# An opening that walks over k with normalised values at once, gate columns with token-major values, GLA states by one scan, and tiles at multiples of 256 bytes

## The chip, the cores and the metric

The kernel is one program on one core of a Trainium2 chip. The metric is the device time of one execution in microseconds (us). Of the kernel before, three runs took 1600.69, 1602.25 and 1602.29 us; their median is 1602.25 us.

## The reference

Two transformer blocks follow one another on 512 tokens (S) of width 1024 (D), all in fp32. The part that the change touches is the beginning of the first block:

```
mod = silu(c) @ ada_w + ada_b            # 6 x 1024: shift, scale, gain of two halves
sh_t, sc_t, g_t, sh_c, sc_c, g_c = split(mod)
h = rms_norm(x, tm_pre_g) * (1 + sc_t) + sh_t
y = token_mixer(h, w_in, ...)
x = x + g_t * rms_norm(y, tm_post_g)
h = rms_norm(x, cm_pre_g) * (1 + sc_c) + sh_c
x = x + g_c * rms_norm(conv_ffn(h, ...), cm_post_g)

token_mixer:  p = h @ w_in               # split in columns:
  mLSTM (q, k, v, o: 256 each; i, f: 4 each)
  GLA   (q, k, v, r: 256 each; a: 16):  log_a = log_sigmoid(a @ w_a2 + bias) / 16
        chunked: state = decay * state + k_dec^T v ; o = q_dec state + masked(q k^T) v
  conformer convolution (512: value and gate), short convolution (3 x 256)
  4 x 1024 gates; merged = sum of gate * (branch @ its output matrix); merged @ w_o
```

The second block (pooling, sparse attention over keys that an indexer picks, a second FFN with a convolution, a last norm) is the same in both kernels.

## The kernel before

**Numbers and products.** The values stand feature-major: 128 features on the partitions, 512 tokens along the row, 8 such blocks for the 1024 features. A product in fp32 is made of three in the faster fp32r format: every weight tile of 128x1024 is loaded raw (512 KB), rounded to `hi` by ScalarE (L120), and the rest `lo = raw - hi` is made by VectorE (L121); the activations have such a pair too (`hh`, `hl`). `mm3` then issues three matmuls: hi with hh (L132), hi with hl (L133), lo with hh (L134). One column block of 128 output columns is 8 blocks of k times 3, so 24 matmuls of 128x512.

**Order.** The program is written as a sequence; a framework with priorities orders each engine's instructions when the program is built, and they run in that order on each engine. `wload` gives loads and splits a higher priority, so that they stand ahead of the products; its buffers (`raw`, `hi`, `lo`) are three deep. SyncE issues all DMAs one after the other; where a buffer isn't free yet, the queue of SyncE waits, and everything behind it too.

**Opening (L347 to L458).** `c` is broadcast to all partitions by a DMA, and its silu makes `cb`. `ada_st(i)` loads a 128x1024 piece of ada_w into one of four `sraw` buffers and reduces it against `cb` on VectorE (L358), which gives 128 values of mod. A first loop over the 8 blocks j of k loads scale piece `ada[8+j]`, x and one weight column block, makes `gcols` (gain times 1+scale) and the pair xg = x times gain, not normalised and without shift, and multiplies it with the first four column blocks (gq0, gq1, gk0, gk1), whose splits stay in `wst`. The row sums of x squared run beside it (ScalarE squares, VectorE adds, L392); `rx`, the reciprocal root of every token's mean, is there after the eighth x, and scales these four results afterwards. A second loop loads the shift pieces `ada[j]`, makes the real h (L439 to L441), and multiplies it with the next four blocks (ifa, ca0, cg0, ca1); one shift piece (j = 1) is reduced by matmuls instead of VectorE (L433). The shift that the first four blocks lack is made by 16 matmuls of the shift with `wst` (L450, L451), and added later from `shw`.

**Gates, GLA and mLSTM.** The column block `ifa` holds 4 columns of i, 4 of f and 16 of a. From it come `i_sb`, `b_sb`, `d_sb` (mLSTM) and log_a (GLA), by Abs, Exp and Ln on ScalarE. The values gv and mv are made token-major, by 96 matmuls of 128x256 each (`gemm_t`, L158). For each p of two (two heads), the states of GLA's 16 chunks are a chain on VectorE: 15 operations of 128x64 (L615, L617), each on the one before. `vx` are copies of v by chunk (VectorE, L605).

**Post.** After the product with w_o the class `Post` adds up squares and products for the post-norm (L291 to L305), with working tiles `sq` of three rows.

## Time and profile before

| | |
|---|---|
| median of 3 runs | 1602.25 us |
| the profiled execution: time, span | 1601.86 us, 1600.1 us |
| mean granted clock of TensorE, as a share of full speed | 0.995 |
| PE, DVE, ACT, POOL busy | 98%, 67%, 42%, 1% |
| mean DMA rate | 110 GB/s |

The span runs from the first to the last instruction; 1.76 us of the execution lie around it. PE is TensorE, DVE VectorE, ACT ScalarE, POOL GpSimd, SP SyncE. A matmul's duration in the trace holds its way through the pipeline, and matmuls overlap; what a matmul costs in a row of them is the distance between two starts. A busy share over the whole span says little of a single stage, so the table is read together with the same shares in short stretches.

### The profile page before, as it was taken

How to read it: one execution, taken by the hardware profiler on the slowest of the kernel's cores; microseconds unless marked ns; L12 is line 12 of the kernel's file. 1: busy time of each engine (PE TensorE's matmuls, PEld its weight loads, DVE VectorE, ACT ScalarE, POOL GpSimd, SP SyncE). 2: the span in 40 equal slices, each digit the busy share in tenths (PEclk: the TensorE clock that was granted, in tenths of full speed). 3: DMA queues.
4: the chain of work that ended last, by engine and by line, in shares of the span. 5: the costliest groups of instructions: out<-in, count | busy, mean ns of one | idle time of the engine just before them, and what ended most of it. 6: DMA issues, size and time to landing. Idle time of an engine off the chain costs nothing.

```text
span 1600.1 us, 20699 instructions
## 1 busy us (share of the span) xinstructions
PE 1567.1 (98%) x8015; PEld 1314.9 (82%) x8015; DVE 1073.7 (67%) x1928; ACT 674.7 (42%) x1028; POOL 16.2 (1%) x43
## 2 busy tenths in 40 slices
PE   6999999999999999999999999999999999999998
PEld 4778888888888988888899978888889988888886
DVE  7776896657768766565358899977556565665234
ACT  4366532223453543443244363448343444444122
POOL 0000100000000000000000000000000000000000
PEclk9999999999999999999999999999999999999999
DMA  8411335544541222223345212220241232232231
GB/s 307 169 53 65 108 119 184 184 167 155 178 146 41 80 92 103 95 93 96 98 132 171 94 67 87 85 93 27 80 154 58 79 101 98 92 105 80 98 113 53
DMA packets 50962, 175.90 MB, mean 110 GB/s; under 512 B 5920, under 2 KB 6192, under 8 KB 50864
## 3 DMA queue, kind: packets, MB, share of 16 engines
q1 hardware_dynamic: 50864, 174.58, 32.7%
q8 instruction: 63, 1.03, 0.3%
q14 instruction: 35, 0.29, 0.1%
HBM read 172.46 MB, written 2.10 MB: 109 GB/s over the span
## 4 chain that ended last, share of the span: by engine, by line
PE 90%; DVE 5%; ACT 2%; issue 1%; DMA 1%; SPq 0%; ACTq 0%; DVEq 0%
PE acc L132 22%; PE acc L133 22%; PE acc L134 22%; PE acc L198 3%; PE acc L1361 3%; PE tp L1361 2%; PE acc L158 1%; PE pc L1270 1%; PE pa L1361 1%; PE pb L1361 1%; PE pc L1361 1%; PE pa L198 1%; PE pb L198 1%; PE pc L198 1%; DVE lo L121 1%
## 5 line engine op out<-in xcount | busy, mean ns | idle before, releaser
L121 DVE TENSOR_TENSOR lo<-raw,hi 128x1024 fp32r<-128x1024 f32 (+1 forms) x245 | 296.4, 1210 | 326.1 <-ACT hi L120 315.8
L132 PE MATMUL acc<-hh,hi 128*128 128x512 f32 x1208 | 473.4, 392 | 0.0
L134 PE MATMUL acc<-hh,lo 128*128 128x512 f32 x1208 | 473.2, 392 | 0.0
L133 PE MATMUL acc<-hl,hi 128*128 128x512 f32 x1208 | 471.8, 391 | 0.0
L120 ACT ACTIVATE hi<-raw 128x1024 fp32r<-128x1024 f32 (+1 forms) x245 | 257.3, 1050 | 477.9 <-PE acc L133 360.8
L132 PEld LDWEIGHTS acc<-hh,hi 128*128 128x128 f32 x1208 | 227.1, 188 | 48.9 <-issue 2.2
L134 PEld LDWEIGHTS acc<-hh,lo 128*128 128x128 f32 x1208 | 227.2, 188 | 47.9 <-issue 0.9
L133 PEld LDWEIGHTS acc<-hl,hi 128*128 128x128 f32 x1208 | 227.1, 188 | 47.8 <-issue 1.4
L134 PE MATMUL acc<-act_h,lo 128*128 128x256 f32 (+1 forms) x242 | 80.3, 332 | 0.0
L133 PE MATMUL acc<-act_l,hi 128*128 128x256 f32 (+1 forms) x242 | 80.2, 331 | 0.0
L132 PE MATMUL acc<-act_h,hi 128*128 128x256 f32 (+1 forms) x242 | 80.1, 331 | 0.0
L120 ACT ACTIVATE act_h<-ffe 128x512 fp32r<-128x512 f32 x44 | 27.7, 630 | 104.2 <-DVE ffe L986 104.2
L268 DVE SCALAR_TENSOR_TENSOR raw<-raw,cb 128x1024 f32<-128x1024 f32 x32 | 39.1, 1223 | 36.7 <-DMA raw<-in_ada_dram 36.6
L982 DVE SCALAR_TENSOR_TENSOR ffe<-acc,vec,ffe 128x510 f32<-128x510 f32 x82 | 61.2, 748 | 2.6
L985 ACT ACTIVATE ffe<-ffe 128x512 f32<-128x512 f32 x44 | 27.8, 631 | 79.6 <-DVE ffe L982 79.6
L980 DVE SCALAR_TENSOR_TENSOR ffe<-acc,vec,ffe 128x511 f32<-128x511 f32 x82 | 60.7, 743 | 0.0
L133 PEld LDWEIGHTS acc<-act_l,hi 128*128 128x128 f32 x242 | 46.0, 190 | 4.4
L134 PEld LDWEIGHTS acc<-act_h,lo 128*128 128x128 f32 x242 | 46.0, 190 | 4.3
L132 PEld LDWEIGHTS acc<-act_h,hi 128*128 128x128 f32 x242 | 46.0, 190 | 4.2
L121 DVE TENSOR_TENSOR act_l<-ffe,act_h 128x512 fp32r<-128x512 f32 x44 | 30.4, 690 | 27.3 <-ACT act_h L120 27.3
L819 DVE SCALAR_TENSOR_TENSOR cv<-u,vec,cv 128x512 f32<-128x512 f32 x60 | 43.3, 745 | 0.0
L198 PE MATMUL acc<-hh,hi 128*128 128x256 f32 x144 | 40.4, 287 | 0.8 <-ACT hh L945 0.7
(635 smaller groups left out, 2752.0 us busy)
## 6 DMA issues: line engine op xcount, KB each, us to landing
raw<-in_up_dram SPq DMA_DIRECT2D x88, 512.0 KB, 3.2
raw<-in_wg_dram SPq DMA_DIRECT2D x48, 512.0 KB, 3.3
raw<-in_dn_dram SPq DMA_DIRECT2D x44, 512.0 KB, 3.5
raw<-in_w_dram SPq DMA_DIRECT2D x43, 512.0 KB, 3.4
raw<-in_ada_dram SPq DMA_DIRECT2D x32, 512.0 KB, 3.3
sraw<-in_ada_dram SPq DMA_DIRECT2D x16, 512.0 KB, 5.7
raw<-in_wo_dram SPq DMA_DIRECT2D x16, 512.0 KB, 3.3
raw<-in_dn_dram SPq DMA_DIRECT2D x11, 384.0 KB, 3.4
```

The lines of the kernel that those rows point to most:

```text
L120: A.activation(hi, src, AF.Copy)
L121: V.tensor_sub(lo, src, hi.bitcast(F32))
L132: T.matmul(out, wh_, ah, start=start, stop=False)
L133: T.matmul(out, wh_, al, start=False, stop=False)
L134: T.matmul(out, wl_, ah, start=False, stop=stop)
L198: T.matmul(a, w_, x_, start=(k == 0 and n == 0 and half == 0), stop=(k == KT - 1 and n == 2 and half == 1), skip_group_check=True)
L268: V.scalar_tensor_tensor(raw, raw, 1.0, cb, op0=ALU.mult, op1=ALU.mult, accum_out=mod[:, i:i + 1])
L819: V.scalar_tensor_tensor(cv[:, j], u0[:, j, k:k + 512], htap[:, 2 * k + j:2 * k + j + 1], cv[:, j], op0=ALU.mult, op1=ALU.add)
L980: V.scalar_tensor_tensor(t[:, 1:512], acc[:, 0:511], vcol(taps, 44 + i), t[:, 1:512], op0=ALU.mult, op1=ALU.add)
L982: V.scalar_tensor_tensor(t[:, 2:512], acc[:, 0:510], vcol(taps, i), t[:, 2:512], op0=ALU.mult, op1=ALU.add)
L985: A.activation(e[0], e[0], AF.Silu)
L1361: T.matmul(o, act[a][:, k, t], w[:, n0:n1], start=(k == 0 and i == 0), stop=(k == KF - 1 and i == 2), skip_group_check=True)
```

## The change

It has four parts.

1. **Opening.** A second copy of x, token-major (`xr`, four pieces of 128x1024, 512 KB each), is loaded first. ScalarE squares its rows with an accumulator, so the row sums `s0` come without VectorE, and `rx` is there before any product. `c` is spread over the partitions by 8 transposes on TensorE and not by a DMA. TensorE multiplies a tile of zeros (`warm`, 3 and 18 matmuls, and 3 on `rx`) in the meantime. `late1`, a one that depends on `rx`'s root, is an operand of the first two reductions. Then one loop over k: per step `ada[8+j]`, x, `ada[j]` and one weight tile are loaded. The weight tile now holds 128 rows of k for all eight column blocks (gq0, gq1, gk0, gk1, ca0, cg0, ca1, cg1), and its 24 matmuls go into eight PSUM banks. h is the final one from the start, so the shift's matmuls, `shw`, `wst`, the second loop and the reduction by matmuls go.
2. **Gate columns.** `ifa` isn't a column block any more; its 24 columns are appended to gv: `wgv`, 96 matmuls of 128x280, and four transposes bring the 24 columns back to feature-major. Exp and Ln run once over three rows.
3. **GLA.** The chain of 15 operations per p becomes one scan over 1024 elements (L593 of the changed kernel) on operands that ScalarE lays out; half of the `vx` copies go to ScalarE. The functions `states`, `chunk_scores`, `gla_out`, `gla_gate` are called in a new order, with the products mq, mk ahead of the GLA work, and gr, mv between its parts.
4. **Tiles.** Many tiles are allocated at multiples of 64 elements (256 bytes); `raw` is 1120 and `hi`, `lo` are 1152 long; `Post` after w_o uses ordinary 128x512 tiles and no `sq3`, and in the first FFN `sq3` has one buffer and not two.

```diff
@@ opening
-        nc.sync.dma_start(out=cb, in_=io["c"].broadcast_to([128, D]))
         nc.sync.dma_start(out=vec[:, 0:VSTART], in_=io["vec"][:, 0:VSTART])
-        A.activation(cb, cb, AF.Silu)
+        nc.sync.dma_start(out=ident, in_=io["cst"])
+        xr = st.tile([128, 4, 1024], F32, name="xr")
+        for b in range(4):
+            nc.sync.dma_start(out=xr[:, b], in_=io["xr"][b * 128:(b + 1) * 128])
+        def warm(n, x_):
+            for _ in range(n):
+                T.matmul(idle[:, 0:x_.shape[1]], ident if x_ is not zero else zero[:, 0:128], x_, start=True, stop=True)
+        warm(WARM[0], zero)
...
+        for n in range(2):
+            cp = bank(("pb", "pc")[n])
+            for k in range(4):
+                T.transpose(cp[:, k * 128:(k + 1) * 128], ccol[:, 4 * n + k:4 * n + k + 1].to_broadcast([128, 128]), ident)
...
+        warm(WARM[1], zero)
+        for b in range(4):
+            A.activation(xr[:, b], xr[:, b], AF.Square, accum_out=s0[:, b:b + 1])
+        y0 = rsqrt(s0, 1.0 / D, 4)
+        late1 = sm.tile([128, 49], F32, tag="late1", name="late1", bufs=1)[:, 0:1]
+        V.tensor_scalar(late1, y0[:, 0:1], 0.0, 1.0, op0=ALU.mult, op1=ALU.add)
+        rb = rowcast(y0)
+        A.activation(rx, rb, AF.Copy)
+        warm(3, rx[:, 0:256])
+        accs = [bank(t) for t in ("acc", "acc", "acc", "pc", "pa", "pb", "tp", "tp")]
+        for j in range(KT):
+            g, sh = gcols[:, 0, j:j + 1], mod[:, j:j + 1]
+            ada_st(8 + j, late1 if j == 0 else 1.0)
             nc.sync.dma_start(out=x0[:, j], in_=io["xT"][:, j])
...
+            ada_st(j, late1 if j == 0 else 1.0)
+            floor[0] = tc.cur_priority
+            w = wload(io["w1"][j])
             V.scalar_tensor_tensor(g, mod[:, 8 + j:9 + j], scb1[:, j:j + 1], vcol("tm_pre_g", j), op0=ALU.add, op1=ALU.mult)
+            V.tensor_tensor(sh, sh, vcol("ada_b", j), op=ALU.add)
             t = st.tile([128, 512], F32, tag="nt", name="nt", bufs=2)
+            V.scalar_tensor_tensor(t, x0[:, j], g, rb if j == 0 else rx, op0=ALU.mult, op1=ALU.mult)
             A.activation(h[0][:, j], t, AF.Identity, bias=sh)
             V.scalar_tensor_tensor(h[1][:, j], t, sh, h[0][:, j].bitcast(F32), op0=ALU.add, op1=ALU.subtract)
+            for m in range(NST):
+                sl = slice(m * 128, (m + 1) * 128)
+                mm3(accs[m], w[0][:, sl], w[1][:, sl], h[0][:, j], h[1][:, j], j == 0, j == KT - 1)
...
-            T.matmul(shp[0:2], shs[:, j], wk[0], start=(j == 0), stop=False, skip_group_check=True)
-            T.matmul(shp[0:1], shs[:, j, 0:1], wk[1], start=False, stop=(j == KT - 1), skip_group_check=True)
@@ gate columns
+        gemm_t([io["wgv"][n] for n in range(2)], h, [o[:, 0:NGV] for o in out], NGV)
...
+        for b in range(4):
+            T.transpose(ifa[0:80, b * 128:(b + 1) * 128], gt4[:, b], ident)
...
+        A.activation(rows[:, 2:5], rows[:, 2:5], AF.Exp, scale=-1.0)
+        A.activation(rows[:, 2:5], rows[:, 2:5], AF.Ln, bias=1.0)
@@ GLA
-                            V.scalar_tensor_tensor(sc_[:, cc + 1], sc_[:, cc], fcol[:, p, cc:cc + 1], kv[:, bi, c],
-                                                   op0=ALU.mult, op1=ALU.add)
+                A.activation(sc_[:, :, 8 * b2:8 * b2 + 8], kv.rearrange("p b c v -> p v (b c)"), AF.Copy)
+            fz = m4("fz")[:, 0:1024]
+            A.activation(fz.rearrange("p (v c) -> p v c", c=16), fcol[:, p].unsqueeze(1).to_broadcast([128, 64, 16]), AF.Copy)
+            V.tensor_tensor_scan(scf, fz, scf, 0.0, op0=ALU.mult, op1=ALU.add)
...
+        states(0)
+        chunk_scores(0)
+        ggate = [gla_gate(j) for j in range(2)]
+        gla_out(0)
+        states(1)
+        chunk_scores(1)
...
+        gemm_t([io["w1"][m], io["w1"][m + 1]], h, [out[b // 2][:, b % 2] for b in range(4)], 256)
...
+        gla_out(1)
@@ tiles
+    def padded(pool, shape, dtype=F32, **kw):
+        return pool.tile([shape[0], (shape[1] + 63) // 64 * 64], dtype, **kw)[:, 0:shape[1]]
-        raw = wr.tile([128, 1024], F32, tag="raw", name="raw")
+        raw = wr.tile([128, 1120], F32, tag="raw", name="raw")
-        post = Post(t2, lambda: m4("sq3")[:, 0:768].rearrange("p (n t) -> p n t", n=3), sums, x, y, gcols[:, 1])
+        post = Post(t2, None, [t2("th", 4) for _ in range(3)], x, y, gcols[:, 1])
-        post = Post(fe, lambda: f1.tile([128, 3, 256], F32, tag="sq3", name="sq3", bufs=2), sums, x, y, gcols[:, 3])
+        post = Post(fe, lambda: f1.tile([128, 3, 256], F32, tag="sq3", name="sq3", bufs=1), sums, x, y, gcols[:, 3])
```

How this moves instructions is seen in three places of the order of the engines.

TensorE at the start of the program, before (`wst` are the kept splits of the first column block, in the first loop):

```order
L132 MATMUL acc<-hh,wst_109 128x512
L133 MATMUL acc<-hl,wst_109 128x512
L134 MATMUL acc<-hh,wst_110 128x512
L132 MATMUL acc<-hh,wst_109 128x512
L133 MATMUL acc<-hl,wst_109 128x512
```

The same place of the changed kernel:

```order
L374 MATMUL acc<-zero 128x256 x5
L385 MATMUL pb<-cst,ccol 128x128 x4
L385 MATMUL pc<-cst,ccol 128x128 x4
L374 MATMUL acc<-zero 128x256 x16
L251 MATMUL tp<-cst,rs_y 128x128 x4
L374 MATMUL acc<-rx,cst 128x256 x3
L134 MATMUL acc<-hh,hi 128x512 x3
L134 MATMUL pc<-hh,hi 128x512
L134 MATMUL pa<-hh,hi 128x512
L134 MATMUL pb<-hh,hi 128x512
```

Ahead of the first product there now stand 21 matmuls on zeros (in two groups), the transposes that spread `c`, the four that spread the reciprocal roots, and three matmuls on `rx`.

VectorE in one step of the second loop, before (L358 is the reduction of a piece of ada_w, L439 to L441 make h):

```order
L437 TENSOR_TENSOR mod<-mod,vec 128x1
L439 SCALAR_TENSOR_TENSOR nt<-x_101,gcols,raw 128x512
L358 SCALAR_TENSOR_TENSOR sraw,mod<-sraw,cb 128x1024
L441 SCALAR_TENSOR_TENSOR hl<-nt,mod,hh 128x512
L437 TENSOR_TENSOR mod<-mod,vec 128x1
```

VectorE from the root's last operation to the end of the first step, after (L359 is the reduction, L123 the split of the weight):

```order
L237 SCALAR_TENSOR_TENSOR rs_y<-rs_u,rs_y 128x4
L398 TENSOR_SCALAR late_168<-rs_y 128x1
L359 SCALAR_TENSOR_TENSOR sraw,mod<-sraw,late_168,cb 128x1024 x2
L411 SCALAR_TENSOR_TENSOR gcols<-mod,scb_117,vec 128x1
L412 TENSOR_TENSOR mod<-mod,vec 128x1
L414 SCALAR_TENSOR_TENSOR nt<-x_101,gcols,tp 128x512
L123 TENSOR_TENSOR lo<-raw,hi 128x1024
L416 SCALAR_TENSOR_TENSOR hl<-nt,mod,hh 128x512
```

A step now has two reductions and a split where the old second loop had one reduction, and the first step's reductions stand behind the root.

VectorE among the states of GLA, before (L617 is one link of the chain, L605 a copy of v):

```order
L615 COPY x1a<-pc 128x64
L605 COPY x1a<-gv 32x2x64
L617 SCALAR_TENSOR_TENSOR x1a<-x1a,fcol,pc 128x64
L605 COPY x1a<-gv 32x2x64
L617 SCALAR_TENSOR_TENSOR x1a<-x1a,fcol,pc 128x64
```

The corresponding place after (L593 is the scan):

```order
L584 COPY x1a<-gv 32x2x64 x4
L695 TENSOR_TENSOR mx_548<-x2a,mx_548 4x512
L603 COPY_PREDICATED x2a<-x2a,pa 128x512
L603 COPY_PREDICATED x2a<-x2a,pb 128x512
L584 COPY x1a<-gv 32x2x64 x4
L593 SCALAR_TENSOR_TENSOR x1a<-fz,x1a 128x1024
L123 TENSOR_TENSOR lo<-raw,hi 128x1024
L634 SCALAR_TENSOR_TENSOR th<-th,acc 128x512
```

The links of the chain are gone from the sequence, and one instruction stands in their place, ahead of which the mask copies of the scores now lie.

## Rows read from the trace of the kernel before

**Rows 1.** The page's list of busy time, share and instructions by engine.
```profile
PE 1567.1 (98%) x8015; PEld 1314.9 (82%) x8015; DVE 1073.7 (67%) x1928; ACT 674.7 (42%) x1028; POOL 16.2 (1%) x43
```

**Rows 2.** Stretches of the span: length, busy time of each engine, clock, DMA share, rate.
```profile
core 0: us, PE busy (x) PEld busy (x) DVE busy (x) ACT busy (x) POOL busy (x), PEclk, DMA share, GB/s
0.00:9.50 9.50, 0.00 (x0) 0.00 (x0) 1.62 (x4) 3.47 (x5) 3.08 (x9) 1.00 0.76 234
8.00:22.00 14.00, 8.07 (x17) 4.53 (x18) 12.38 (x20) 9.49 (x14) 0.00 (x0) 1.00 1.03 405
20.00:40.00 20.00, 18.05 (x81) 13.50 (x81) 19.09 (x47) 9.82 (x14) 0.00 (x0) 1.00 0.82 289
40.00:60.00 20.00, 18.38 (x75) 15.18 (x74) 17.83 (x33) 5.16 (x8) 0.00 (x0) 0.83 0.60 218
...
100.88:112.94 12.06, 9.74 (x41) 6.05 (x40) 9.96 (x26) 4.62 (x9) 0.00 (x0) 0.72 0.25 87
...
180.00:200.00 20.00, 20.00 (x96) 16.62 (x95) 19.96 (x38) 11.13 (x17) 0.00 (x0) 1.00 0.50 175
```

**Rows 3.** Timeline of PE: start, duration, operation; the opening, and full clock later.
```profile
11.68 0.80 PE L132 MATMUL acc<-hh,wst 128*128 128x512 f32 x1 [11.68 <-ACT wst L120]
...
17.38 0.63 PE L132 MATMUL acc<-hh,wst 128*128 128x512 f32 x1
17.80 0.63 PE L133 MATMUL acc<-hl,wst 128*128 128x512 f32 x1
...
200.10 0.39 PE L133 MATMUL acc<-hl,hi 128*128 128x512 f32 x1
200.33 0.39 PE L134 MATMUL acc<-hh,lo 128*128 128x512 f32 x1
```

**Rows 4.** Timeline of PE, end of the opening to the values gv.
```profile
72.52 0.40 PE L450 MATMUL tp<-wst,sh 128*2 128x512 f32 x1
...
82.33 1.98 PE L551 MATMUL tp<-rows,wa 16*128 16x512 f32 x4
84.24 0.39 PE L158 MATMUL acc<-hi,hh 128*128 128x256 f32 x1
...
95.86 0.40 PE L132 MATMUL acc<-hh,hi 128*128 128x512 f32 x1
```

**Rows 5.** Timeline of DVE, one step of the second loop.
```profile
51.40 0.15 DVE L437 TENSOR_TENSOR mod<-mod,vec 128x1 f32<-128x1 f32 x1
51.47 0.74 DVE L439 SCALAR_TENSOR_TENSOR nt<-x,gcols,raw 128x512 f32<-128x512 f32 x1
52.13 1.22 DVE L358 SCALAR_TENSOR_TENSOR sraw<-sraw,cb 128x1024 f32<-128x1024 f32 x1
...
53.94 0.15 DVE L437 TENSOR_TENSOR mod<-mod,vec 128x1 f32<-128x1 f32 x1
```

**Rows 6.** The page's group of the split on DVE, all over the span.
```profile
L121 DVE TENSOR_TENSOR lo<-raw,hi 128x1024 fp32r<-128x1024 f32 (+1 forms) x245 | 296.4, 1210 | 326.1 <-ACT hi L120 315.8
```

**Rows 7.** Timeline of ACT: a 1024-element and a 512-element operation.
```profile
43.86 1.06 ACT L120 ACTIVATE hi<-raw 128x1024 fp32r<-128x1024 f32 x1 [3.32 <-DMA raw<-in_w_dram]
44.82 0.71 ACT L440 ACTIVATE hh<-nt,mod 128x512 fp32r<-128x512 f32 x1
```

**Rows 8.** Timeline of DVE: two neighbours in a reciprocal root, and a scan.
```profile
488.13 0.16 DVE L230 TENSOR_TENSOR rs_u<-rs_y 128x2 f32<-128x2 f32 x1
488.32 0.16 DVE L231 SCALAR_TENSOR_TENSOR rs_u<-rs_u,rs_s 128x2 f32<-128x2 f32 x1
...
95.81 1.20 DVE L559 TENSOR_TENSOR_SCAN e<-x2a,tmp 128x512 f32<-128x512 f32 x1
```

**Rows 9.** DMA issues of the first 60 us: size and median us to landing.
```profile
sraw<-in_ada_dram SPq DMA_DIRECT2D x16, 512.0 KB, 5.7
```

**Rows 10.** GLA: PE's wait for the decayed values, and DVE's chain of states by line.
```profile
103.47 0.71 PE L628 MATMUL pa<-e 64*128 64x128 f32 x4 [2.21 <-DVE e L575]
...
L617 DVE SCALAR_TENSOR_TENSOR x1a<-x1a,fcol,pc x28: 261/281/282, 112.8 to 136.3; 128x64 f32<-128x64 f32 x28
```

More of the change, by code (lines that the diff above doesn't have):

```diff
@@ L157, in gemm_t @@
                     for m, (a, x_) in enumerate(((ah, w[0]), (ah, w[1]), (al, w[0]))):
-                        T.matmul(out[b], a, x_[:, k], start=(q == 0 and m == 0 and b * n % 512 == 0),
+                        T.matmul(out[b], a, x_[:, k], start=(q == 0 and m == 0 and b % (512 // n) == 0),
                                  stop=(q == KT - 1 and m == 2), skip_group_check=True)
@@ L453, in block_kernel @@
-        A.activation(shr, shp[0:2], AF.Copy)
-        tp = bank("tp")
-        for m in range(NF):
-            T.transpose(tp[:, 2 * m:2 * m + 2], shr[:, m * 128:(m + 1) * 128], ident[0:2, 0:2])
-        shw = sm.tile([128, NF], F32, tag="shw", name="shw", bufs=1)
-        V.tensor_reduce(shw, tp[:, 0:2 * NF].rearrange("p (m n) -> p m n", n=2), axis=AX.X, op=ALU.add)
+            if j == 4:
+                load_consts()
+            for m in range(NST):
+                sl = slice(m * 128, (m + 1) * 128)
+                mm3(accs[m], w[0][:, sl], w[1][:, sl], h[0][:, j], h[1][:, j], j == 0, j == KT - 1)
@@ L459, in block_kernel @@
+        for j in range(2):
+            A.activation(gq[:, j], accs[j], AF.Copy, scale=0.125)
+        for j in range(2):
+            A.activation(gk[:, j], accs[2 + j], AF.Copy)
         dump("h1", h[0].bitcast(F32))
-    pend = dict(zip(MT1[NF:NST], accs[NF:]))
+    pend = dict(zip(MT1[4:NST], accs[4:]))
     floor[0] = tc.cur_priority
@@ L475, in acc_of @@
             return gemm(io["w1"][MT1.index(name)], h)
-        def tok256(name):
-            m = MT1.index(name + "0")
-            out = [bank("acc").rearrange("p (b n) -> p b n", b=2) for _ in range(2)]
-            gemm_t([io["w1"][m], io["w1"][m + 1]], h, [out[b // 2][:, b % 2] for b in range(4)])
-            return out
-        ifa = acc_of("ifa")
-        rows = p1.tile([128, 3, 512], F32, tag="rows", name="rows")
-        gx = rows[:, 0]
-        A.activation(gx[64:80], ifa[64:80], AF.Copy)
-        i_sb, b_sb, d_sb = (rows[0:4, n] for n in range(3))
+        rows = p1.tile([128, 5, 512], F32, tag="rows", name="rows")
+        G.memset(rows[:, 2], 0.0)
         mx2 = p1.tile([128, 512], F32R, name="mx2")
@@ new lines, in block_kernel @@
+        ifa = bank("tp")
+        for b in range(4):
+            T.transpose(ifa[0:80, b * 128:(b + 1) * 128], gt4[:, b], ident)
+        gx, fm, fa = (rows[:, n] for n in range(3))
+        gf = gx[32:36]
+        i_sb, b_sb, d_sb = (rows[0:4, n] for n in range(3))
+        fb = vec[32:36, VOFF["if_bias"]:VOFF["if_bias"] + 1]
+        A.activation(gx[64:80], ifa[64:80], AF.Copy)
+        A.activation(fa[32:36], ifa[32:36], AF.Abs, bias=fb)
+        V.tensor_scalar(gf, ifa[32:36], fb, 0.0, op0=ALU.add, op1=ALU.min)
@@ new lines, in block_kernel @@
+        A.activation(i_sb, ifa[0:4], AF.Identity, bias=vec[0:4, VOFF["if_bias"]:VOFF["if_bias"] + 1])
+        gab = rows[:, 3:5]
+        gmn = m4("gmn")[:, 0:1024].rearrange("p (j t) -> p j t", j=2)
+        for j in range(2):
+            u = bank(("pa", "pb")[j])
+            T.matmul(u, wa2[64:80, j * 128:(j + 1) * 128], gx[64:80])
+            A.activation(gab[:, j], u, AF.Abs, bias=vcol("gla_a_bias", j))
+            V.tensor_scalar(gmn[:, j], u, vcol("gla_a_bias", j), 0.0, op0=ALU.add, op1=ALU.min)
@@ L530, in block_kernel @@
+        A.activation(rows[:, 2:5], rows[:, 2:5], AF.Exp, scale=-1.0)
+        A.activation(rows[:, 2:5], rows[:, 2:5], AF.Ln, bias=1.0)
+        V.tensor_sub(gmn, gmn, gab)
+        V.tensor_sub(fm[32:36], gf, fa[32:36])
+        V.tensor_copy(d_sb, fm[32:36])
+        for dst, nm in ((mq, "mq"), (mk, "mk")):
+            for j in range(2):
+                A.activation(dst[:, j], acc_of(f"{nm}{j}"), AF.Copy)
+        cx = padded(p1, [128, 514], name="cx")
         x1 = yp.tile([128, 4096], F32, tag="y", name="x1a")
@@ L634, in block_kernel @@
                 for hh in range(2):
-                    T.matmul(o[:, b, hh * 64:hh * 64 + 64], ats[hh][:, b], gv[:, b, p * 128 + hh * 64:p * 128 + hh * 64 + 64],
+                    T.matmul(o[:, b, hh * 64:hh * 64 + 64], atz[hh][:, b], gv[:, b, p * 128 + hh * 64:p * 128 + hh * 64 + 64],
                              start=(b == 0 and hh == 0), stop=False, skip_group_check=True)
+            for b in range(4):
                 for c in range(4):
@@ L1189, in block_kernel @@
         pump(PUMP_V0)
-        gemm_t([io["w2"][m + n] for n in range(4)], h, vb)
+        gemm_t([io["w2"][m + n] for n in range(4)], h, vb, 512)
         for b in range(4):
```

298 lines of the change are left out of this document (102 added, 196 removed).

## The prediction

> **What bounds the kernel now.** I read the list of busy times first: TensorE is busy 98% [rows 1], so time can come only from matmuls that go, or from places where TensorE waits or runs slowly. The table of stretches says where these are. From 180 us on a stretch of 20 us holds 20.00 us of busy TensorE at full clock [rows 2]; before that TensorE stands still until 11.68 us [rows 3], is busy 18.05 and 18.38 us of 20 in the two following stretches, the latter at a granted clock of 0.83, and in 100.88 to 112.94 us it waits and has a clock of 0.72 [rows 2]. The change lies in just this part.
>
> The timeline of TensorE gives the price of a matmul: 128x512 in a row start 0.227 us apart (200.10, 200.33, rounded) at the full 2.4 GHz, and 0.43 us apart (17.38, 17.80) at the start, which is the spacing of the lower level, 1.2 GHz [rows 3]. A column block of 24 costs 24 x 0.227 = 5.44 us. Eight blocks are 43.5 us; before, they take from 11.68 [rows 3] to 72.52 us [rows 4], 60.8 us, so 17.3 us there are waits, slow clock and small matmuls. It is a feed problem: VectorE is busy 19.09 of 20 us and 17.83 of 20 [rows 2].
>
> **Opening: when the first product starts.** The base of the sum is the profiled execution, 1601.86 us, span 1600.1; it lies 0.4 us under the median of the runs. TensorE's first product needs rx, which needs all of xr. Ahead of and with xr lie 44 KB, 64 KB and four times 512 KB, 2.2 MB; before moves 234 GB/s x 9.5 us = 2.2 MB in its first 9.5 us [rows 2], so xr is there at about 9.5 us. (With 405 GB/s from 2 us on it would be 7.5.) Then in series: the last square on ScalarE 1.06 [rows 7] and its sum, estimated 0.2; the root with late1, 11 small operations at 0.19 us from start to start [rows 8], 2.1; two reductions of ada_w, 2 x 1.2 [rows 5]; two column operations, 0.3; nt 0.74 [rows 5]; hh 0.71 [rows 7]. That is 9.5 + 1.3 + 2.1 + 2.4 + 0.3 + 1.5 = 17.1. Starting and passing on between engines I estimate at 0.6: first product at 17.7 us, 6 later than before. TensorE's own queue ahead of it (21 matmuls on zeros, transposes, three on rx) is fp32: two such products of 512 columns take 1.9 us (82.33 to 84.24 [rows 4]), four times an fp32r one, so 256 columns take 0.45 us at full clock and 0.86 at the lower spacing. Begun at some 1.4 us, the matmuls on zeros and the transposes end by about 15.5 us, ahead of h, so the chain above decides; bounds for the start 15.2 (xr early) to 20.5 us (a warm-up queue wholly at the low spacing).
>
> **Opening: the pace of a step.** A step has TensorE 5.44 us of matmuls. VectorE: the old step of the second loop takes 53.94 - 51.40 = 2.54 us [rows 5]; a second reduction adds 1.14 to 1.22 [rows 5], the split 1.2 [rows 6], a column operation 0.13: 5.1. ScalarE: 1.06 + 0.71 [rows 7]. DMA: three loads of 512 KB and one of 256 KB, 1.835 MB: 4.5 us at the 405 GB/s that 8 to 22 us show, 6.35 at the 289 of 20 to 40 us, 8.4 at the 218 of 40 to 60 us [rows 2]. The two low rates belong to stretches in which VectorE, holding the buffers, was full or the loads few, so I take the first: TensorE is the bound, with 0.35 us over VectorE. The eight steps end at 17.7 + 43.5 + 0.3 (what a step slips by) = 61.5 us. I read whether VectorE's 0.35 us holds as the weakest joint here; at 5.8 us instead of 5.1 it would cost 7 x 0.35 = 2.5 us.
>
> The Trainium skill, TensorE: Matmul & The Clock Gate, section "Wait — 56ns, not 53.3ns?", gives 215.7 ns from start to start for warm matmuls of 512 columns; by this figure the 192 matmuls would need 41.4 us and not 43.5. The trace has 0.227 in its undisturbed stretch [rows 3], and the trace decides.
>
> **Opening: what stands behind it.** The 16 matmuls for the shift, from 72.52 us on [rows 4], the block ifa (5.44 us) and the reduction by matmuls go, all contained in the mark that I use: the end of gv. Before it is 95.86 us [rows 4]. gv takes (95.86 - 84.24)/96 = 0.121 us per matmul of 256 columns; 280 columns in proportion are 0.132, 96 of them 12.7 us. After, gv ends at 61.5 + 12.7 = 74.2: 21.7 us sooner. But before has the two products with w_a2 (1.9 us, 82.33 to 84.24 [rows 4]) ahead of the mark, and after has them behind it, with four fp32 transposes of 128 columns, 0.5 by the pace of those same products. **Gain 19.3 us.** Bounds by the start (15.2 to 20.5) and the pace (5.44 to 6.35 us a step): 10 to 22.
>
> **GLA and mLSTM.** Before, TensorE waits 2.2 us for the decayed values [rows 10], and the clock falls behind that wait: 0.28 x 12.06 = 3.4 us [rows 2]. Together 5.6. After, the products mq, mk stand between the products with w_a2 and the first use of the decayed values: four blocks less a few matmuls that run ahead, 89 x 0.227 = 20.2 us of cover. The chain that they must cover: two Abs, Exp and Ln over 1536 elements, two scans of 1.20 [rows 8], six to eight operations of 512 elements at 0.7 and the splits of the four weights on VectorE [rows 6]; by these rows I add up to 20.6 us. So a wait of about half a us stays there, another of some 0.5 at the transposes of the decayed keys, and about 0.8 where the second half's copies stand between the root's operations: 1.8, too short to take the clock as the 2.2 us did. **Gain 3.8 us**, bounds -5 (the cover misses by 9 us with the clock gone) to 5.6.
>
> The states themselves gain nothing by their own length. The old chain is 14 links x 0.28 us = 3.9 us per p [rows 10]; the scan of 1024 elements, twice the 1.20 of 512 [rows 8], is 2.4, and the copies that lay out its operands on ScalarE are another 1.06 to 2.1 [rows 7]. What changes is that products stand beside it: gr ahead of the first output, mv ahead of the second. Later the convolution taps on VectorE start some 20 us sooner with the whole sequence, so the gates behind them don't become late.
>
> **Tiles and Post.** Fewer and smaller pieces of work lie between w_o and the FFN; at that transition two splits move out of VectorE's crowded part (2 x 1.2 us of VectorE [rows 6]) and 8 additions become shorter but more, which I value at **0.5 us**, bounds 0 to 2. Whether a tile that begins at a multiple of 256 bytes reads faster no row shows; the matmuls in rows 3 already run evenly, so I take 0, bounds -1 (the larger tiles' order) to +3. From 500 us on every engine has the same order as before, so nothing is lost or won there.
>
> **Sum.** 19.3 + 3.8 + 0.5 = 23.6; 1601.86 - 23.6 = **1578.3 us**. Own range of this case: 1573 to 1583.
>
> **Rivals.**
>
> *The matmuls on zeros do not raise the clock, or it falls before the first product.* For it: the low level lasted from 11.68 to at least 17.80 us in before although products had begun [rows 3], and no row shows a matmul on zeros. Against it: they fill some 14 us. Price: one episode, as in 100.88 to 112.94 us, 3.4 us [rows 2]. Time 1581.7. Chance 12%. The Trainium skill (same page, section "Part 1: The HAM clock gate") says that the throttled state is the default and activity releases it; the two levels agree with the spacings in rows 3, and whether zeros are activity no run here shows.
>
> *The loads bound the opening.* At 289 GB/s [rows 2] a step is 6.35 us, 7 x 0.91 = 6.4 us lost: 1584.7. For it: the 1.03 share of DMA at 405 GB/s leaves nothing above, and a step needs 337. Chance 13%.
>
> *New waits in the GLA part.* The chain of Exp, Ln, scans and products is longer than its cover by some 4 us, TensorE waits and the clock falls as in before: 4 + 3.4 less the 0.5 that I count already: 7, time 1585.3. For it: 20.6 against 20.2 us is no margin, and a wait of 2.2 us did take the clock [rows 2, 10]. Chance 12%.
>
> *The opening becomes a serial loop, and the kernel slower.* Both reductions of a step use the four sraw buffers; SyncE's queue waits for a free one, and x, the weights and everything behind wait with it. If only one step's loads can be under way while the step before is reduced, a step is 5.7 (landing [rows 9]) + 5.1 (VectorE) = 10.8 us, 7 x 5.3 = 37 us lost: 1615. It decides from 5.44 + 23.6/7 = 8.8 us a step on. Against it: four buffers hold two steps, so a load has about 10 us to land. Chance 4%.
>
> *More is won than counted.* The start at 15.2, no wait in GLA and the tiles worth 3 us: 2.5 + 1.8 + 3 = 7.3 more, 1571. Chance 4%.
>
> The forecast keeps 55%. All but the serial loop (and mishaps together, 1%) end faster than before by over 0.2%, which is 3.2 us and about what a measurement of this kernel can tell from no change. Faster 0.93, within it 0.02, slower 0.05. The range reaches from the better case's middle, 1569, over the feed and the GLA rival with some of both, to 1592.
>
> **What the profile of the changed kernel will show.** The first product (a 128x512 matmul) starts at 17 to 18.5 us at a spacing of 0.227 at once; 0.43 there speaks for the clock rival. Eight steps of 5.4 to 5.6 us, TensorE without waits over 0.3 us until about 61.5 us, VectorE some 93% busy; steps of 6.3 us with TensorE waiting for ScalarE's or VectorE's work on late loads speak for the feed. gv ends near 74 us. The wait ahead of the score matmuls is under 1 us, and the granted clock has no stretch under 1.00 between 60 and 180 us. If TensorE's clock or a wait shows up after 180 us where before has none, or if the first product starts after 21 us, the forecast is wrong in a step that I have not priced.

## The result, and the profile after

The changed kernel takes 1580.96 us, the median of four runs (1578.87 to 1582.23), against 1602.27 us of before; the ratio is 0.9871 with a 95% interval of 0.9855 to 0.9888. It is 21.3 us faster; 23.6 were forecast, and 1578.3 us. The time lies in the range and in the likeliest case's own. That the sum came out so near is in part luck, since errors stood against each other: the GLA part lost 2.8 us where 3.8 were to be won, and three other terms brought 4.9 us more than was counted for them.

The profiled execution has a span of 1578.2 us, 21.9 less than before; TensorE is busy 99% of it.

The stretches of the span of the changed kernel, with the columns of [rows 2]:

```profile
20.00:40.00 20.00, 20.00 (x90) 16.57 (x89) 19.96 (x43) 7.73 (x9) 0.00 (x0) 1.00 1.03 405
40.00:60.00 20.00, 20.00 (x90) 16.55 (x89) 17.13 (x28) 9.02 (x13) 4.19 (x9) 1.00 0.76 255
...
100.00:120.00 20.00, 16.27 (x66) 11.37 (x67) 11.97 (x28) 10.55 (x18) 0.00 (x0) 0.83 0.13 41
...
180.00:200.00 20.00, 18.59 (x86) 15.14 (x86) 19.76 (x38) 8.09 (x13) 0.00 (x0) 1.00 0.47 157
```

TensorE is busy without a gap from 20 to 60 us, where before had 18.05 and 18.38 of 20, the second at a granted clock of 0.83 [rows 2]. The loads run at 405 GB/s in the first of these stretches, the rate that the forecast took. But 100 to 120 us is no better than the stretch from 100.88 us was before: TensorE is idle for 3.7 us, and the clock is 0.83. The stretch of 180 to 200 us, which was full, has lost 1.4 us.

The timeline of TensorE, from the matmuls on zeros to the end of gv (rows that answer to [rows 3, 4]; the trace has two records for each of these fp32 matmuls, so x10 and x32 are the 21 matmuls on zeros):

```profile
1.20 4.64 PE L374 MATMUL acc<-zero 128*128 128x256 f32 x10 [1.20 <-POOL zero L369]
...
6.64 7.07 PE L374 MATMUL acc<-zero 128*128 128x256 f32 x32
...
14.84 1.56 PE L374 MATMUL acc<-rx,cst 128*128 128x256 f32 x6 [0.69 <-ACT rx L400]
17.20 0.97 PE L134 MATMUL acc<-hh,hi 128*128 128x512 f32 x3 [0.80 <-ACT hh L415]
...
18.70 0.40 PE L135 MATMUL acc<-hl,hi 128*128 128x512 f32 x1
18.93 0.39 PE L136 MATMUL acc<-hh,lo 128*128 128x512 f32 x1
...
60.88 0.29 PE L159 MATMUL acc<-hi,hh 128*128 128x280 f32 x1
...
73.25 0.49 PE L485 MATMUL tp<-cst,ga 128*80 128x128 f32 x3
```

The first ten records on zeros take 0.46 us each, the later 32 take 0.22: by the second group the clock had come to its upper level. The first product starts at 17.20 us, and but for the first three, 0.27 us apart, the spacing is 0.23 us at once. The eight blocks end at 60.88: 43.7 us for 43.5 forecast. gv is done at 73.25 us.

Where the 21.9 us came from is best read by counting the matmuls from the end of the program, and comparing their starts in the two traces. The order is the same from about 500 us on. At the other places counted, what is left to do is the same work, but at "gates, early" the changed kernel has already done an fp32 matmul on the conformer's sums that before does at 364 us, about 0.5 us more work:

| place | start before | start after | sooner by |
|---|---|---|---|
| end of gv (by name) | 95.86 | 73.25 | 22.6; 20.2 with the 2.4 us of work moved behind it |
| ahead of the gates | 217.10 | 199.66 | 17.4 |
| gates, early | 262.54 | 246.11 | 16.4 |
| gates, late | 432.81 | 414.63 | 18.2 |
| ahead of the FFN | 487.67 | 469.42 | 18.3 |
| in the FFN | 509.20 | 488.46 | 20.7 |
| second block | 858.84 | 838.07 | 20.8 |
| later in the second block | 1257.70 | 1235.78 | 21.9 |

So the opening and the gate columns brought 20.2, the stretch with GLA, mLSTM and the short convolution took 2.8, the gates brought 0.8 and the way to the FFN another 0.1, the way from w_o into the FFN 2.4, and the second block 1.2. The gates' 0.8 is what is left after a wait of 0.6 us for a weight split at 230 us, which before does not have.

The list of TensorE's waits from 70 to 200 us names the loss (engine, tile, line, whom it waited for, us in total, times, the longest):

```profile
PE tp L588 <- DVE x1a L584: 3.8, 2, 2.8
PE acc L134 <- ACT th L790: 1.4, 1, 1.4
PE pc L588 <- ACT e L564: 1.3, 1, 1.3
PE pa L732 <- DVE x2a L736: 1.1, 1, 1.1
PE acc L134 <- ACT th L788: 0.8, 1, 0.8
```

The longest one, in TensorE's timeline:

```profile
102.13 0.27 PE L601 MATMUL pa<-e 64*128 64x128 f32 x1
105.23 1.12 PE L588 MATMUL tp<-x1a,e 128*64 128x256 f32 x4 [2.83 <-DVE x1a L584]
...
109.81 0.63 PE L134 MATMUL acc<-hh,hi 128*128 128x512 f32 x1
110.23 0.63 PE L135 MATMUL acc<-hl,hi 128*128 128x512 f32 x1
```

And what VectorE did meanwhile:

```profile
97.64 1.04 DVE L656 TENSOR_TENSOR_SCAN rows<-x2a,rows 4x128 f32<-4x128 f32 x3
...
102.39 0.68 DVE L667 TENSOR_TENSOR rows<-rows,x2a 4x512 f32<-4x512 f32 x1
103.00 1.21 DVE L123 TENSOR_TENSOR lo<-raw,hi 128x1024 fp32r<-128x1024 f32 x1
104.13 0.96 DVE L584 COPY x1a<-gv 32x128 f32<-32x128 f32 x4
```

TensorE waits for the four copies of v (L584). They overwrite a buffer that the first half's products read until 102 us. In VectorE's order they stand behind the small operations of mLSTM (L656 to L667) and a weight split, and start at 104.13, some 2 us after the buffer is free. Behind the wait the products are 0.43 us apart: the clock is at its lower level until about 111.5 us.

### The profile page after: what moved, and what is told of

It reads as the page before. It is cut to its first block, busy times and chain, and to the rows that moved or that the text cites. A ratio compares the mean times of both kernels' runs of the same rounds, so it can differ in the third digit from the quotient of the medians.

```text
span 1578.2 us, 20647 instructions
## 1 busy us (share of the span) xinstructions
PE 1555.6 (99%) x8007; PEld 1314.9 (83%) x8007; DVE 1057.2 (67%) x1887; ACT 675.7 (43%) x1035; POOL 18.3 (1%) x47
## 4 chain that ended last, share of the span: by engine, by line
PE 91%; DVE 5%; ACT 2%; issue 1%; DMA 1%; SPq 0%; DVEq 0%; ACTq 0%
PE acc L134 22%; PE acc L135 22%; PE acc L136 22%; PE acc L199 3%; PE acc L1347 3%; PE acc L159 2%; PE tp L1347 2%; PE pc L1256 1%; PE pa L1347 1%; PE pb L1347 1%; PE pc L1347 1%; PE pa L199 1%; PE pb L199 1%; PE pc L199 1%; DVE lo L123 1%
## 5 line engine op out<-in xcount | busy, mean ns | idle before, releaser
L123 DVE TENSOR_TENSOR lo<-raw,hi 128x1024 fp32r<-128x1024 f32 (+2 forms) x249 | 301.7, 1212 | 331.0 <-ACT hi L122 327.2
L122 ACT ACTIVATE hi<-raw 128x1024 fp32r<-128x1024 f32 (+2 forms) x249 | 261.9, 1052 | 434.6 <-PE acc L135 294.6
L123 DVE TENSOR_TENSOR act_l<-ffe,act_h 128x512 fp32r<-128x512 f32 x44 | 30.4, 692 | 27.3 <-ACT act_h L122 27.3
L199 PE MATMUL acc<-hl,hi 128*128 128x256 f32 x144 | 40.8, 285 | 0.1
```

The source lines that it names most:

```text
L122: A.activation(hi, src, AF.Copy)
L123: V.tensor_sub(lo, src, hi.bitcast(F32))
L199: T.matmul(a, w_, x_, start=(k == 0 and n == 0 and half == 0), stop=(k == KT - 1 and n == 2 and half == 1), skip_group_check=True)
```

## The experiments

Times are medians. The ratios to the kernel before, with their intervals, are given where the verdict needs them. Edits are shown in part; `...` marks what is left out. The opening differs by up to 0.8 us even between two profiles of one kernel, so a gain read from a trace is given net of that where it matters.

**The opening without warm-up.**

```diff
-WARM = (3, 18)
+WARM = (0, 0)
...
-        warm(3, rx[:, 0:256])
```

> The changed kernel without the 21 matmuls on zeros and the three on rx; all results the same. Theory 1 (the warm-up buys the full clock for the first steps): the first 128x512 products start at about 17.2 us as before, but 0.43 us apart instead of 0.227, and the granted clock comes up some 7 to 8 us later; cost 3.4 to 4 us, about 1584.5. Rival (the clock would be up anyway, because the transposes and early loads suffice, or the opening has enough slack elsewhere): products at 0.227 from the first on, time within 1 us of 1581.

Measured: 1583.16 us, ratio 0.9889 (0.9873 to 0.9905), 2.2 us slower than the changed kernel by the medians; the intervals overlap, and the trace decides. TensorE's timeline:

```profile
17.05 1.65 PE L134 MATMUL acc<-hh,hi 128*128 128x512 f32 x3 [3.33 <-ACT hh L414]
...
18.93 0.63 PE L134 MATMUL pa<-hh,hi 128*128 128x512 f32 x1
19.35 0.63 PE L134 MATMUL pb<-hh,hi 128*128 128x512 f32 x1
...
22.17 0.39 PE L135 MATMUL pc<-hl,hi 128*128 128x512 f32 x1
22.39 0.39 PE L136 MATMUL pc<-hh,lo 128*128 128x512 f32 x1
```

The first product starts at 17.05, 0.15 us earlier, but until about 22 us the products are 0.42 us apart. The column of the granted clock reads 1.00 here for 16 to 22 us all the same, as it does for 8 to 22 us in [rows 2], so in the opening the level has to be read from the spacing. The loss in the opening is 2.1 to 2.3 us, counted on the same matmuls up to 310 us; theory 1 holds with a smaller price than 3.4 to 4, since the low clock lasts 5 us here. Another 1.7 us of this profile's 3.8 are lost at 356 us, where the edit has no part (last section).

**Small tiles at their exact length.**

```diff
-        return pool.tile([shape[0], (shape[1] + 63) // 64 * 64], dtype, **kw)[:, 0:shape[1]]
+        return pool.tile([shape[0], shape[1]], dtype, **kw)
```

> The changed kernel with small tiles (vec, cst, mod, gcols, s0, m4, cx, fcol, mi, gs, dcol, sel, rc, wq) at their exact length again and not at multiples of 256 bytes. Theory 2 (what a matmul reads at an address off the 256-byte grid streams slower): the products with boh and bol go from 0.227 to 0.232 to 0.235 us apart and the stretch of the gates takes 1.5 to 2 us longer, the second block about 1 us, in all +2 to +3.5 us, about 1583.5. Rival (the gain of that stretch comes from the new order of buffers or from Post, not from addresses): spacing stays 0.227, time within 0.7 us of the changed kernel.

Measured: 1583.56 us (1582.33 to 1583.70, every run above every run of the changed kernel), 2.6 us slower by the medians, the profiled span 3.7 us longer. The products with boh and bol in the gates, first of the changed kernel, then of this one:

```profile
389.69 0.39 PE L134 MATMUL acc<-boh,hi 128*128 128x512 f32 x1
...
390.37 0.39 PE L134 MATMUL acc<-boh,hi 128*128 128x512 f32 x1
```

```profile
391.80 0.40 PE L134 MATMUL acc<-boh,hi 128*128 128x512 f32 x1
...
392.50 0.40 PE L134 MATMUL acc<-boh,hi 128*128 128x512 f32 x1
```

From one product hi with boh to the next are three products; they take 0.68 us in the one and 0.70 in the other, 3% more. By the count of matmuls the gates lose 1.9 us against the changed kernel and the second block 1.4, both spread evenly over their products; the remaining 0.6 us arise before 20 us. Theory 2 holds. The instructions and their order are the same, only where tiles lie differs; that it is the offset from the 256-byte grid, and not another property of the place, was not separated.

**Two more buffers for the copies of v.**

```diff
+        gmf = gmn.rearrange("p j t -> p (j t)")
+        G.memset(gmf, 0.0)
+        vx += [gmf[:, 512 * n:512 * n + 512].rearrange("p (h c v) -> p h c v", h=2, c=4) for n in range(2)]
...
+                v0 = 2 if p == 0 and b2 == 1 else 0
...
-                            V.tensor_copy(vx[bi][r, :, c, :], src)
+                            V.tensor_copy(vx[v0 + bi][r, :, c, :], src)
...
```

> The changed kernel with two more buffers for the chunked copies of v (in the tile gmn, free by then), so that the second half's copies for p = 0 need not wait for the first half's products, and stand ahead of the mLSTM scans on VectorE. Theory 3 (the 2.8 us wait of TensorE at 102.4 us is for four copies queued behind the mLSTM scans and a split, and the clock falls because of it): the wait goes and so does the stretch of low clock; gain 2.8 + 3.4 = 6 us where all of it counts, 1575; at least 3. Rival (behind the copies another operation is just as late: the transposed keys, the laying out of the scan's operands, or the weight splits): the wait moves to the next place and the gain is under 1.5 us.

Measured: 1574.59 us, ratio 0.9833 (0.9818 to 0.9848), 6.4 us faster than the changed kernel and clear of it. VectorE's timeline, and then TensorE's:

```profile
98.13 0.68 DVE L588 COPY gmn<-gv 32x128 f32<-32x128 f32 x3
98.85 1.36 DVE L660 TENSOR_TENSOR_SCAN rows<-x2a,rows 4x128 f32<-4x128 f32 x4
```

```profile
101.29 1.08 PE L592 MATMUL pc<-x1a,e 128*64 128x256 f32 x8 [1.16 <-ACT e L567]
102.18 1.06 PE L592 MATMUL tp<-gmn,e 128*64 128x256 f32 x8
```

The copies now stand ahead of mLSTM's scans, the second half's products follow the first's without a wait, and the granted clock of 100 to 120 us is 1.00 (it was 0.83). By 115 us of the changed kernel's trace 6.1 us are won, and they are all still there at the end. This profile's opening is 0.6 us later than the changed kernel's, so the edit's own share is 6.7 us; the second profile of the same kernel (last experiment) gives 6.7 as well. Theory 3 holds in full; no other operation took the wait's place.

**Busy matmuls in the wait.**

```diff
+HOLD = 12
...
+                if p == 0 and b2 == 1:
+                    kvf = kv.rearrange("p b c v -> p (b c v)")
+                    for n in range(HOLD):
+                        T.matmul(kvf[:, 0:128], ident, ident, start=True, stop=True)
```

> The changed kernel with 12 fp32 matmuls of the identity on itself (128x128) put on TensorE right ahead of the products that wait 2.8 us at 102.4 us; their result is overwritten. The wait stays, TensorE is busy in it. Theory 3 (the fall of the clock is a price of its own on top of the wait): the granted clock stays 1.00 in 100 to 120 us and the time falls by 2.5 to 3.4 us, about 1578. Rival (the clock falls for the sparse products around it, or the low stretch is hidden because VectorE and ScalarE set the pace there): the clock still falls, or the time stays within 1 us of 1581.

Measured: 1578.98 us, ratio 0.9860 (0.9845 to 0.9875). By the medians that is 2.0 us faster, less than was expected, and the intervals overlap with those of the changed kernel: two of the four runs took 1577 us, the other two 1581. The profile is one of the quicker two, so what follows is shown for that execution alone. It is 3.4 us ahead of the changed kernel at 120 us (3.1 net of an opening that is 0.3 us earlier), and 2.8 at the end. The stretch of TensorE (columns: length, busy, clock, DMA share, GB/s) and its timeline:

```profile
100.00:120.00 20.00, 19.11 (x134) 1.00 0.17 55
```

```profile
101.62 2.94 PE L589 MATMUL tp<-cst 128*128 128x128 f32 x24
104.85 1.08 PE L593 MATMUL tp<-x1a,e 128*64 128x256 f32 x8 [0.29 <-DVE x1a L585]
```

The second half's products start 3.2 us after the first half's have ended, so the wait is there, filled; the clock stays up. The wait and the fall of the clock are therefore two prices: about 3.1 us for the clock, and 3.6 for the wait, which is what is left of the 6.7 of the experiment before. The two runs of 1581 us, whose mean clock is 0.996 to 0.997 where the other two have 0.999, may have had a fall after all; where, no trace shows. Theory 3 holds in the profile, and by the medians it stays unclear.

**The new opening alone, in the kernel before.** The edit puts in the opening that the change has; shown is only what differs from it.

```diff
...
-MT1 = ["gq0", "gq1", "gk0", "gk1", "ifa", "ca0", "cg0", "ca1", "cg1", "gv0", "gv1",
+MT1 = ["gq0", "gq1", "gk0", "gk1", "ca0", "cg0", "ca1", "cg1", "ifa", "gv0", "gv1",
...
-            V.scalar_tensor_tensor(gq[:, j], gq[:, j], shw[:, j:j + 1], e, op0=ALU.add, op1=ALU.mult)
+            V.tensor_tensor(gq[:, j], gq[:, j], e, op=ALU.mult)
...
```

> The kernel before with the new opening alone: ifa is an ordinary column block behind the eight, gv has 256 columns, the chain of states, the order of the GLA part, the tiles and Post are those of before. Theory A (the opening is worth what the mark at the end of the eight blocks says, and hands it on whole): the eight blocks end at about 61 us, ifa at 66.4, gv at about 80 against 95.86, and the program ends 14 to 17 us sooner, about 1586; the other three parts together bring the missing 5 us. Rival (the GLA part of before eats some of it, because what VectorE and ScalarE owe there is not done sooner by as much): the mark after GLA is less than 11 us ahead, time about 1591 or more.

Measured: 1587.78 us, ratio 0.9912 (0.9893 to 0.9931), 14.0 us faster than the runs of before beside it. TensorE's timeline:

```profile
68.11 1.98 PE L515 MATMUL tp<-rows,wa 16*128 16x512 f32 x4
...
71.59 0.41 PE L155 MATMUL acc<-hi,hl 128*128 128x256 f32 x1
71.81 0.41 PE L155 MATMUL acc<-hi,hh 128*128 128x256 f32 x1
...
81.69 0.40 PE L129 MATMUL acc<-hh,hi 128*128 128x512 f32 x1
...
85.46 1.43 PE L592 MATMUL pa<-e 64*128 64x128 f32 x5 [2.68 <-DVE e L539]
```

gv ends at 81.69, 14.2 us ahead of before's 95.86 [rows 4], and 14.3 of it are still there at 200 us. About 80 was expected: from 71.2 to 74.6 us gv's products are 0.21 us apart and not 0.12, which costs some 1.5 us. At 488 us the clock falls once more, and 13.1 us are left at the end. Theory A holds, at the low end of its 14 to 17: here too the GLA part waits, 2.7 us for the 2.2 of before [rows 10]. The other three parts bring the remaining 6.8 us (1587.78 to 1580.96).

**The new Post alone, in the kernel before.**

```diff
...
-        sums = p1.tile([128, 3, 512], F32, name="sums")
-        post = Post(t2, lambda: m4("sq3")[:, 0:768].rearrange("p (n t) -> p n t", n=3), sums, x, y, gcols[:, 1])
+        post = Post(t2, None, [t2("th", 4) for _ in range(3)], x, y, gcols[:, 1])
```

> The kernel before with only the new Post after w_o (four 128x256 additions on single tiles where a half had three rows added at once; the tile sums goes, th has four buffers). Theory B (the two weight splits g1l leave VectorE's crowded 490 to 510 us, and TensorE's waits for g1h, act_h and hh there go): gain 2 to 2.5 us, all of it between 480 and 512 us, about 1599.9. Rival (the 2.4 us there come from tiles or from the time at which loads land): no gain in that stretch, time within 0.7 us of before.

Measured: 1598.17 us, ratio 0.9979 (0.9966 to 0.9991), 3.6 us under the runs of before beside it. Before waits for the late splits at 500 and 503 us (TensorE's timeline of before):

```profile
499.92 0.39 PE L198 MATMUL pa<-hh,g1h 128*128 128x256 f32 x1 [0.63 <-ACT g1h L120]
...
503.34 0.38 PE L198 MATMUL pc<-hh,act_h 128*128 128x256 f32 x1 [0.56 <-ACT act_h L120]
```

Before makes the two splits g1l at 500.5 and 503.2 us. With the new Post they are made at 471 and 476 us, ahead of the crowd (VectorE's timeline):

```profile
471.08 1.23 DVE L121 TENSOR_TENSOR g1l<-raw,g1h 128x1024 fp32r<-128x1024 f32 x1 [0.36 <-ACT g1h L120]
475.76 1.22 DVE L121 TENSOR_TENSOR g1l<-raw,g1h 128x1024 fp32r<-128x1024 f32 x1
```

No wait stands in TensorE's timeline from 480 to 512 us, and 2.7 us are won there, counted on the same matmuls. Theory B holds; whether the shorter additions have a share in it was not separated from the splits. The other 0.9 us of this profile's 3.5 arose before 130 us, where the edit has no part, and is a matter of the clock: in 40 to 60 us, where before has 0.83 [rows 2], this execution has 1.00 and is 2.7 us ahead behind it, and in 100 to 120 us it has 0.74 and loses part of that again.

**The chain of states instead of the scan, in the changed kernel.**

```diff
...
-            V.tensor_tensor_scan(scf, fz, scf, 0.0, op0=ALU.mult, op1=ALU.add)
...
+                            V.scalar_tensor_tensor(sc_[:, cc], sc_[:, cc - 1], fcol[:, p, cc:cc + 1], kv[:, bi, c],
+                                                   op0=ALU.mult, op1=ALU.add)
```

> The changed kernel with the states of GLA by the chain of 15 operations per p again, straight from PSUM, in the new order of the functions and with everything else of the change; no scan, no laying out of its operands by ScalarE. Theory C (the scan brings nothing by itself, the order with products beside it does): the 2.8 us wait and the low clock stay, time within 1 us of the changed kernel, 1580 to 1582. Rival (the scan is what makes the GLA part short): the outputs of GLA wait for the chain, 3 us or more slower, 1584. A third possibility: ScalarE's strided copies cost more than the chain does, 1 to 3 us faster.

Measured: 1579.51 us, ratio 0.9864 (0.9843 to 0.9884), no difference. On the same matmuls it is within 0.3 us of the changed kernel from 130 to 340 us. Later 2.2 us go at 352 us, 0.7 by a wait for ScalarE and the rest by a fall of the clock behind it (last section). The scan brings nothing by itself (theory C).

**The keys' copies ahead on ScalarE, with the two buffers.** The transposes and copies of the keys are put at a higher priority.

```diff
+PRIO = 400
...
-            tokens(ktok[:, :, j * 128:(j + 1) * 128], kf[:, j])
+            with tc.high_priority(offset=PRIO):
+                tokens(ktok[:, :, j * 128:(j + 1) * 128], kf[:, j])
...
```

> The kernel with two more buffers for the copies of v, and the token-major copies of the decayed keys ahead of a weight split, a copy of mk and the laying out of fcol on ScalarE. Theory D (the 1.2 us wait ahead of the first state products and the 1.0 us behind it are queues on ScalarE and VectorE of the same kind): both go, gain about 2 us over the version with the buffers alone, 1572.5. Rival (the decayed keys themselves are late, or the split that is now behind them becomes the wait): under 0.7 us.

Measured: 1576.42 us, ratio 0.9838 (0.9816 to 0.9861); the profile is 2.6 us slower than the first one with the buffers alone. Theory D fell in this form: the priority also moved the transposes forward in TensorE's order, to a place where the keys were not ready (TensorE's timeline):

```profile
95.45 0.87 PE L567 MATMUL tp<-cst,e 128*128 128x128 f32 x4 [2.73 <-DVE e L558]
```

**Two places in ScalarE's order only.** The priority now holds for the copies alone, and for the short convolution's bg and cg.

```diff
-            A.activation(dst, tp.rearrange("p (b c) -> p b c", b=4), AF.Copy)
+            with tc.high_priority(offset=PRIO):
+                A.activation(dst, tp.rearrange("p (b c) -> p b c", b=4), AF.Copy)
...
+            with tc.high_priority(offset=PRIO):
+                A.activation(cg, r, AF.Copy)
...
```

> The kernel with two more buffers for the copies of v, and ScalarE's copies in two places ahead of what stands before them: the token-major keys ahead of a copy of mk, and the short convolution's copy cg ahead of a weight split and two others. TensorE's own order is meant to stay. Theory D2 (TensorE's waits of 1.2 us for the keys and 1.4 us for the short convolution's bank are each a place in ScalarE's queue): the 1.4 us wait goes and the 1.2 us falls to about 0.6, time 2 us under the version with the buffers alone. Rival (something else is as late in both places): within 0.7 us of it.

Measured: 1573.88 us, ratio 0.9820 (0.9807 to 0.9833), beside 1573.36 us (0.9819, 0.9806 to 0.9832) of the version with the buffers alone. The rival holds. The wait for the keys is 1.1 us (1.1 and 1.2 in the two profiles with the buffers alone). The wait for the short convolution's bank is half of its 1.4 us (TensorE's waits), but a later one has grown (its timeline):

```profile
PE acc L135 <- ACT th L800: 0.7, 1, 0.7
```

```profile
224.23 0.50 PE L135 MATMUL acc<-hh,hi 128*128 128x512 f32 x1 [1.56 <-ACT hi L123]
```

So 0.7 us were won at 178 us, and at 224 us, where TensorE now waits 1.6 us for ScalarE's rounding of a weight and not 0.6, and at 239 us 1.5 were lost again. That the weight is late because the copies went ahead of such work on ScalarE was not tested.

**The two buffers once more**, beside the one before, without an edit.

> The version with the two more buffers once more, beside the one before it, for the comparison on one chip and to see how steady the stretch of one-column matmuls near 350 us is. Theory 3 says 1573 to 1576 us again, with no low clock between 90 and 120 us. If the clock falls behind the one-column matmuls in this profile and did not in the earlier one of the same kernel, that fall is a matter of the single execution; if it never shows here, it belongs to the kernels in which it showed.

Measured: 1573.36 us, with no low clock between 90 and 120 us, and 0.8 us less in the span than its first profile, all of it from the opening on. Behind the one-column matmuls the clock did not fall in either profile of this kernel. With the version before it, which cannot be told from it, it is the fastest that was run: 7.6 us under the changed kernel and 29.5 under the one before by the medians.

## Why the prediction was right, and where not

*The start of the first product* (17.7): 17.20. Right, and by the terms of the sum: the last square ends at 10.63 us (10.56 in the sum), the root with late1 takes 2.1 us, the two reductions 2.4, nt ends at 16.40 and hh at 17.15. Only the 0.6 us for passing on between engines was too much.

*The pace* (5.44 us a step, TensorE the bound): the eight steps took 43.7 us. VectorE was at 19.96 of 20 us in 20 to 40 us; its step, from one reduction to the same of the next step (its timeline), is 5.0 us for the 5.1 estimated:

```profile
23.12 1.22 DVE L359 SCALAR_TENSOR_TENSOR sraw<-sraw,cb 128x1024 f32<-128x1024 f32 x1
...
28.13 1.22 DVE L359 SCALAR_TENSOR_TENSOR sraw<-sraw,cb 128x1024 f32<-128x1024 f32 x1
```

The weakest joint held; the feed rival did not come, the loads ran at 405 GB/s. The serial loop did not come either.

*The clock* (warm-up holds it): right in the opening, where the matmuls on zeros brought the upper level; without it 2.2 us are lost, for the 3.4 of the rival. Wrong further on, where no stretch under 1.00 was expected from 60 to 180 us and 100 to 120 us has 0.83.

*The opening and the gate columns*: 20.2 us by the mark for 19.3. gv took 12.4 us for 12.7.

*GLA and mLSTM* (gain 3.8): **this step failed; it lost 2.8.** The forecast allowed a wait of 0.8 us where the second half's copies stand, and took its waits together to be "too short to take the clock". The place was right, the queue was not: I had counted the copies behind the root's operations of p = 1, and not those of p = 0 behind the small scans of mLSTM and a split on VectorE, which the order of the changed kernel puts ahead of them. The wait was 2.8 us and took the clock, 6.7 us together by the experiment with the buffers. That is as much as the whole miss: without it the stretch comes to a gain of 3.9. The cover for the decayed values did hold: from the end of the products with w_a2 at 77.4 us the cover lasts 20.3 us for the 20.2 counted, and VectorE's last decayed values are there after 19.2. The 20.6 of the forecast can't be worked out again from the operations that it lists. TensorE waited 1.3 us behind that, for ScalarE's copies and not for the chain. That is the rival of new waits, with its mechanism of wait and clock, at another operation than the one it named. Three later waits of 1.1, 1.4 and 0.8 us were not foreseen at all; halving one of them did not pay, so what stands behind them is open. None of these waits of 1.4 us or less took the clock.

*The states*: nothing by their own length, as the text said; the chain in the scan's place changes nothing.

*Post* (0.5): 2.4 in the profile, 2.7 alone. The mechanism was right and the size was off: two splits of 1.2 us leave the part in which TensorE waited for splits, and as much time is won.

*Tiles* (0, bounds -1 to 3): 3.3 by the profile of the experiment that undoes them (1.9 in the gates, 1.4 in the second block), 2.6 by its medians. Of the 1.9 the gates kept less by the count, with the wait at 230 us between. The statement that from 500 us on nothing is won or lost fell by the 1.2 us of the second block. The rows that I read were products with h, which run at 0.227 us in both; the products with boh and bol, at 0.232 to 0.235 us in before, were not looked at on their own.

The sum: -2.8 instead of 3.8 is 6.6 lost; 0.9 by the opening, 1.9 by Post and 2.1 in the gates and the second block are won beside the forecast. That takes 23.6 to the measured 21.9. The range's lower end is given as the better case's middle, 1569, where that case's own sum is 1571; nothing else hangs on it.

## What to carry to other kernels

Where TensorE is full, a wait costs itself, and it can cost the low clock behind it as well: in the GLA part the clock fell behind waits of 2.2 to 2.8 us (before, after and the experiments that have such a wait), and behind waits of 0.8 to 1.4 us it did not. A buffer that lets the copies be ordered ahead saved both prices; matmuls that fill the wait saved the second in the execution that was profiled. When a change reorders an engine's instructions, read for every operation that another engine waits for what stands directly ahead of it in the new order, and which buffer it reuses. Products on different operands should be read for their spacing one by one: 3% on a part of them was worth 2.6 to 3.3 us here, as much as the new Post.

## What the runs showed that was not expected

A tile's place changes the pace of matmuls that read it: 0.227 against 0.232 to 0.235 us for the same 128x512 product, with no other difference in the program than the length of small tiles.

The clock can fall with almost no wait of TensorE. In the run without warm-up it fell behind eight one-column matmuls (two records each), ahead of which TensorE waits 0.18 us (TensorE's timeline):

```profile
354.79 1.62 PE L244 MATMUL tp<-cst,tmp 128*128 128x1 f32 x14
356.26 0.61 PE L135 MATMUL acc<-hl,hi 128*128 128x512 f32 x1
356.67 0.63 PE L136 MATMUL acc<-hh,lo 128*128 128x512 f32 x1
```

The products behind are 0.43 us apart. The changed kernel's own profile has the same instructions at 352.35 us and full clock behind them. The one with the chain fell there too, behind a wait of 0.7 us; the one with busy matmuls in the wait has 0.6 us of wait at the same place, and no fall. With the opening alone, the products 0.21 us apart at 71.6 us came a little after 2 us of matmuls of 16 rows, with no wait of 0.2 us or more ahead of them; before has the same matmuls at 82.33 us [rows 4], and no slow products behind. The Trainium skill (TensorE: Matmul & The Clock Gate, section "Part 1: The HAM clock gate") says that activity releases the clock and that the number of slow matmuls at the start of one kernel differs from run to run. That a fall in the middle of a kernel differs in the same way is suggested by these profiles, which have the same matmuls there in different kernels; no two profiles of one kernel here show it. The fall at 350 us costs about 1.5 us without the wait ahead of it, close to half of the 3.4 us between the fastest and the slowest run of the changed kernel, but which runs had it is not known, since only one of each kernel was profiled.
